# A two-block network on one core: softmax statistics in a tile for each branch, moved by SyncE; the tail's third tile loaded ahead of weights; a third store buffer

## The chip, the core and the metric

The kernel runs on one core of one Trainium2 chip. The metric is the device time of one execution in microseconds. Engines are named as in the profile: PE (TensorE), DVE (VectorE), ACT (ScalarE), POOL (GpSimd), SP (SyncE, which here only issues DMAs).

## The reference, cut to what matters

Two blocks, one after the other, on 2048 tokens of width 1024. The first has two layers, each with a Fourier mixer, a neighbourhood attention and a gated linear attention (GLA) side by side, and an output projection. The second is a dilated attention beside a gated MLP, an output product and a gated "ple" product:

```python
DILATIONS = ((128, 1), (512, 4), (2048, 16))
def _dilated_attention(q, k, v):                 # 8 heads of 64, 2048 tokens
    outs, lses = [], []
    for window, dilation in DILATIONS:
        o, l = _dilated_branch(q, k, v, window, dilation)   # banded softmax in blocks of 128
        outs.append(o)
        lses.append(l)                                      # m + log(den)
    w = softmax(stack(lses), axis=0)
    return sum(w[..., None] * stack(outs), axis=0)

def second_block(x, p, ...):
    ...
    o_b = _dilated_attention(q, k, v) * silu(gate_b)
    mixed = concatenate([o_b, o_a], axis=-1)                # o_a: gated MLP
    h = h + mixed @ w_out
    gate = sigmoid(_rmsnorm(h, g_ple) @ w_ple_gate + b_ple_gate)
    return h + gate * (p @ w_ple_proj)
```

The maximum m and the denominator den of each branch are per token; a branch of dilation r holds them in the order of its residue classes, so before the branches can be weighed against each other they have to be brought to one order.

## The kernel before

All products are in float32 made of two halves, hi and lo, with three products each (`split` makes the halves: hi on ACT, lo on DVE or POOL). The order of the instructions on each engine is made by a planner: it simulates the program with a cost model, takes instructions in program order where several are ready, and may pull later ones ahead; on the chip each engine then runs its list in order, and each waits for what it needs. In `b2_mid` SP's instructions keep the program's order from the end of the attention's units on (`tc.manual_schedule`).

**Dilated attention** (`b2_attn`, 3558 to 3935 us). Four pairs of heads; in each, three branches (`br` 0, 1, 2) of 16, 14 and 8 units (`n`); two units make a couple. `scores` computes a couple's scores (L1801, L1805), takes the row's extreme on DVE (L1812, into the column m of the statistics tile `ast`) and the Exp with its sum on ACT (L1814, into the column d). `turned` transposes (PE L1822, DVE L1824), `values` multiplies with V (L1838) and ACT stores into `aoT` (L1846); both run one and two couples behind. `gather` moves the statistics of branches 0 and 1 into the order of branch 2: a transpose on PE (L1854), a copy on DVE (L1857), one store `sd<-sts` (L1858) and four stores `sd<-ast` (L1861) to DRAM, and one load `ax<-sd` (L1864), all from POOL; it runs at units 1 and 4 of branch 2. `combine` begins with DVE's L1873, which reads `ax`, makes the weights on POOL (L1883 to L1894), stores them (`wd`, SP, L1895), loads them broadcast (`awb`, `awg`) and weighs and adds the three branches (L1924 to L1927: POOL for the first three pairs, mostly DVE for the last), and stores to `mixT` (L1930). In the program it begins in the next pair, but the planner pulls L1873 into branch 2. The operands of the next pair (`kq`, L1734, and `aV`, L1765 to L1770) are loaded on SP during a pair; 11 `kq` buffers serve five a pair.

**Tail** (`b2_mid`, `Tail`). For 16 tiles of 128 tokens: `products` (L2195, tile of `mixT` times `w_out`), `normed`, `turn` (transposes, L2236), `second` (L2254, times `w_ple_gate`). Weights go through raw buffers and are split. Tiles 0 and 1 have their buffers early, tile 2 gets the twelfth of the slots cut out of `kq` buffers and is loaded after the gate weights W6 and W7; W4, W5 and W0 to W3 of the gate go through two buffers `btr`.

**First block** (`mixers`). GLA steps run with gate units first; when these are done the neighbourhood attention's units (`na`) begin and one of them is drawn with each GLA step. What is left of them runs beside `ple_proj` (L1518 product, L1521 ACT copy into `plst`, L1522 store) and the output projection's weights. `OutProj.begin` then loads the first two tiles `om` (L1410); `products` splits a tile (`left`: `omh` on ACT, `om` on POOL) and multiplies (L1430).

## Time and profile before

| | us |
|---|---|
| median of 3 runs | 4350.35 (4340.16 to 4353.33) |
| the profiled execution | 4348.48 |
| its span | 4346.7 |
| PE busy | 4059.6 (93%) |
| DVE, ACT, POOL busy | 1738.6, 1642.4, 1501.5 |
| DMA, mean over the span | 145 GB/s |

1.8 us of the profiled execution lie outside the span. The mean granted clock of PE is 0.960 of full speed (of its two levels, 1.2 and 2.4 GHz). In a row of a timeline the columns are: start, duration, engine, line, instruction, written tile <- read tiles, shape, count, and in brackets the idle time of the engine just before and what ended it.

### The profile page before, as it was taken

To read this page: it belongs to the slowest core of one execution; us is meant where nothing else is said; L and a number is where in the kernel's file an instruction comes from. 1 tells how busy PE (TensorE), PEld (TensorE's weight loads), DVE (VectorE), ACT (ScalarE), POOL (GpSimd) and SP (SyncE) were. 2 spreads that over 40 slices of the span, in tenths; PEclk is the share of its full clock that TensorE was granted. 3 is DMA by queue.
4 is the path that set the end of the run, shared out by engine and by line. 5 is a ranking of instruction groups with operands and counts; after the bars stand their busy time and mean duration, and the time that the engine had idled before them with its cause. 6 is when DMAs were issued, how large, how long until landed. Compare 5 with 4: busy or idle time off the path is not lost. (4 is left out here: it accounts for less than half of the span.)

```text
span 4346.7 us, 79462 instructions
## 1 busy us (share of the span) xinstructions
PE 4059.6 (93%) x29633; PEld 3491.9 (80%) x29633; DVE 1738.6 (40%) x4996; ACT 1642.4 (38%) x4121; POOL 1501.5 (35%) x1949
## 2 busy tenths in 40 slices
PE   7999999898899999999988989989999989887998
PEld 6988789676677799888967767889998877765887
DVE  5331123477532443112347744544620036555222
ACT  5141233574551332323356554252222126553221
POOL 4234333224222323232321422445723332543433
PEclk9999999898999999999999989999999989888999
DMA  6435454766766444334477574532321267545231
GB/s 207 138 113 150 146 164 155 187 167 182 201 189 209 140 139 128 121 119 158 154 200 180 170 204 157 167 122 78 108 89 49 88 189 175 143 107 162 84 95 63
DMA packets 539035, 629.94 MB, mean 145 GB/s; under 512 B 118504, under 2 KB 417836, under 8 KB 535194
## 3 DMA queue, kind: packets, MB, share of 16 engines
q1 hardware_dynamic: 487546, 477.18, 38.7%
q0 software_dynamic: 39552, 129.60, 9.1%
q10 hardware_dynamic: 11552, 18.08, 1.2%
q8 instruction: 235, 3.85, 0.4%
q14 instruction: 150, 1.23, 0.1%
HBM read 424.26 MB, written 200.41 MB: 144 GB/s over the span
## 5 line engine op out<-in xcount | busy, mean ns | idle before, releaser
L301 PE MATMUL mm<-whi,hTh 128*128 128x304 f32 (+2 forms) x1424 | 420.3, 299 | 1.5 <-ACT hTh L221 1.5
L301 PE MATMUL mm<-wlo,hTh 128*128 128x304 f32 (+2 forms) x1424 | 417.7, 297 | 0.0
L301 PE MATMUL mm<-whi,hTl 128*128 128x304 f32 (+2 forms) x1424 | 381.1, 296 | 0.0
L254 POOL TENSOR_TENSOR wlo<-wraw,whi 128x128 fp32r<-128x128 f32 (+3 forms) x384 | 223.3, 608 | 404.2 <-ACT whi L253 392.1
L301 PE MATMUL mm<-whi,h2h 128*128 128x256 f32 x1024 | 293.1, 290 | 2.2 <-ACT h2h L221 2.2
L301 PE MATMUL mm<-wlo,h2h 128*128 128x256 f32 x1024 | 284.9, 282 | 0.0
L301 PE MATMUL mm<-whi,h2l 128*128 128x256 f32 x1024 | 271.9, 284 | 0.0
L301 PEld LDWEIGHTS mm<-whi,hTh 128*128 128x128 f32 x1424 | 269.1, 189 | 2.8 <-ACT hTh L221 2.0
L301 PEld LDWEIGHTS mm<-wlo,hTh 128*128 128x128 f32 x1424 | 268.9, 189 | 0.0
L301 PEld LDWEIGHTS mm<-whi,hTl 128*128 128x128 f32 x1424 | 257.0, 189 | 1.1 <-issue 1.1
L578 PE MATMUL gps<-gh,whi 128*128 128x256 f32 x816 | 233.4, 286 | 6.0 <-ACT gh L155 6.0
L578 PE MATMUL gps<-gh,wlo 128*128 128x256 f32 x816 | 232.2, 285 | 0.0
L578 PE MATMUL gps<-gl,whi 128*128 128x256 f32 x816 | 231.7, 284 | 0.0
L304 PE MATMUL mm<-hTh,whi 128*128 128x512 f32 x600 | 227.9, 381 | 0.0
L304 PE MATMUL mm<-hTh,wlo 128*128 128x512 f32 x600 | 227.0, 378 | 0.0
L304 PE MATMUL mm<-hTl,whi 128*128 128x512 f32 x600 | 226.4, 377 | 0.0
L1430 PE MATMUL ops<-owh,omh 128*128 128x512 f32 x544 | 215.1, 395 | 4.4 <-ACT omh L155 4.4
L1430 PE MATMUL ops<-owh,om 128*128 128x512 f32 x544 | 212.3, 391 | 2.0 <-POOL om L156 2.0
L1430 PE MATMUL ops<-owl,omh 128*128 128x512 f32 x544 | 212.5, 391 | 0.0
L1814 ACT ACTIVATE ae<-ae,ast 128x256 f32<-128x256 f32 (+1 forms) x384 | 171.1, 448 | 101.6 <-DVE ast L1812 101.6
L253 ACT ACTIVATE whi<-wraw 128x128 fp32r<-128x128 f32 (+3 forms) x416 | 127.3, 357 | 210.2 <-DMA wraw<-in_w_in 172.5
L301 PEld LDWEIGHTS mm<-wlo,h2h 128*128 128x128 f32 x1024 | 196.4, 192 | 0.0
(486 smaller groups left out, 10774.8 us busy)
## 6 DMA issues: line engine op xcount, KB each, us to landing
qkv<-gl SPq DMA_DIRECT2D x72, 384.0 KB
adaw<-in_w_ada SPq DMA_DIRECT2D x48, 512.0 KB
Q<-ql SPq DMA_DIRECT2D x88, 256.0 KB
hl<-evk SPq DMA_DIRECT2D x68, 256.0 KB
gl<-hl SPq DMA_DIRECT2D x17, 1024.0 KB
om<-mixTl SPq DMA_DIRECT2D x34, 512.0 KB
gTl<-ev POOLq DMA_DIRECT2D x67, 256.0 KB, 3.4
wraw<-in_w_in SPq DMA_DIRECT2D x32, 512.0 KB
```

The lines of the kernel that those rows point to most:

```text
L253: nc.scalar.activation(out=hi[:, :C], in_=raw[:, k], func=AF.Copy)
L254: (eng or nc.gpsimd).tensor_tensor(out=lo[:, :C], in0=raw[:, k], in1=f(hi[:, :C]), op=ALU.subtract)
L301: nc.tensor.matmul(ps[:, :C], s.hT[x][:, k, 128 * g:128 * g + 128], w[k][y][:, :C], start=st, stop=sp)
L304: nc.tensor.matmul(ps[:C, :tn], w[k][y][:, :C], s.hT[x][:, k, t0:t0 + tn], start=st, stop=sp)
L578: nc.tensor.matmul(ps.rearrange("p (t n) -> p t n", t=2), W[b][k][y][:, 128 * j:128 * j + 128], h[x][:, :, k], start=n == 0, stop=n == 23)
L1430: nc.tensor.matmul(ps, m[x][:, k], W[k][y][:, 512 * n:512 * n + 512], start=k == j == 0, stop=k == 7 and j == 2)
L1814: nc.scalar.activation(out=e, in_=e, func=AF.Exp, scale=-1.0, bias=m, accum_out=d)
```

## The change

Five edits. (1) The statistics are in one tile for each branch instead of one for all three; `gather` begins at unit 4 of branch 1 with its transpose, its copy and the store of branch 0 come at unit 8 of branch 1, the four stores of branch 1 at unit 2 of branch 2 and the load at unit 5; all its DMAs go from POOL to SP. (2) In the tail the third tile gets its buffer and its two loads right after the first step of weights; W6 alone goes through the old buffers, W7 and W4 go first through `btr`; the third tile is split on DVE at step 3. (3) `plst` has three buffers instead of two. (4) After the first `na` step the next three GLA steps draw no `na` unit; these come later, beside `ple_proj`. (5) `OutProj.first` splits tile 0 at the third of the `na` units that are left after `begin`, instead of in `products`.

```diff
--- before.py
+++ after.py
@@ -1347,13 +1347,16 @@
             left = 3 * ((54 if l == 0 else 48) + 2)
             for i, _ in enumerate(gla):
                 if units is not None:
-                    left -= 1
-                    next(units, None)
+
+                    if i > begun + 3:
+                        left -= 1
+                        next(units, None)
                 elif i % 3 == 2 and [x for x in range(2) if next(gates, 1)]:
                     e2.close()
                     keep.close()
                     units = na(K, A, l, S, B, pool(es, "na", side="right"), pp, (2, 3))
                     next(units)
+                    begun = i
                     pp.tile = pool(es, "naps", space=PSUM, side="right").tile
         next(w)
         with ExitStack() as e1:
@@ -1369,8 +1372,9 @@
                 for _ in x:
                     pass
         proj.begin()
-        for _ in units:
-            pass
+        for i, _ in enumerate(units):
+            if i == 2:
+                proj.first()
 
 
 
@@ -1399,8 +1403,12 @@
 
         s.p1 = s.es.enter_context(s.K.tc.tile_pool(name="opm", bufs=1, reuse_waits="tile"))
         s.ld = {}
+        s.m = {}
         for t in range(2):
             s.load(t)
+
+    def first(s):
+        s.m[0] = s.left(0)
 
     def load(s, t):
         if t >= len(s.tiles):
@@ -1471,7 +1479,7 @@
                 e1.close()
                 if s.ahead is not None:
                     s.ahead()
-            m = s.left(t)
+            m = s.m[t] if t in s.m else s.left(t)
             ps = []
             for n in range(2):
                 ps.append(pp.tile([128, 512], F32, name="ops", tag="ops"))
@@ -1489,7 +1497,7 @@
     W = (p.tile([128, 2, D], F32R, name="plwh"), p.tile([128, 2, D], F32R, name="plwl"))
     for c in range(4):
         cs = slice(256 * c, 256 * c + 256)
-        wr = p.tile([128, 2, 256], F32, name="plwr", tag="plst", bufs=2)
+        wr = p.tile([128, 2, 256], F32, name="plwr", tag="plst", bufs=3)
         nc.sync.dma_start(wr, A["w_ple_proj_2"][0][:, cs].rearrange("(k p) n -> p k n", p=128))
         split(K, W[0][:, :, cs], W[1][:, :, cs], wr)
     ld = {}
@@ -1517,7 +1525,7 @@
                 for a, b in MM3:
                     nc.tensor.matmul(ps, X[a][:, k], W[b][:, k, 512 * n:512 * n + 512], start=j == 0, stop=j == 5)
                     j += 1
-            o = p.tile([128, 512], F32, name="plst", tag="plst", bufs=2)
+            o = p.tile([128, 512], F32, name="plst", tag="plst", bufs=3)
             nc.scalar.activation(out=o, in_=ps, func=AF.Copy)
             nc.scalar.dma_start(ple[128 * t:128 * t + 128, 512 * n:512 * n + 512], o)
             yield
@@ -1783,7 +1791,7 @@
     def scores(pr, br, us, X):
 
 
-        st = X["st"]
+        st = X["st"][br]
         ps = [pp.tile([128, 2, 256], F32, name="aps", tag="aps", bufs=4) for _ in range(2)]
         ecs = [pa.tile([128, 2, 256], F32, name="ae", tag="ae", bufs=4) for _ in us]
         todo = []
@@ -1807,7 +1815,7 @@
             for hh in range(2):
 
                 col = (b, 4 * b + r, r)[br]
-                m, d = (st[:, br, x, hh, col:col + 1] for x in range(2))
+                m, d = (st[:, x, hh, col:col + 1] for x in range(2))
                 e = ecs[i][:, hh, cs]
                 nc.vector.tensor_tensor_reduce(out=e, in0=ps[hh][:, i, cs], in1=band[:, cs if full else slice(128, 256)], scale=1.0, scalar=BIG,
                                                op0=ALU.add, op1=ALU.min, accum_out=m)
@@ -1848,26 +1856,26 @@
     def gather(pr, X):
 
 
-
-        st = X["st"]
         pst = pp.tile([64, 128], F32, name="pst", tag="apo", bufs=2)
-        nc.tensor.transpose(pst, st[:, 0].rearrange("p s h t -> p (s h t)"), K.ident)
+        nc.tensor.transpose(pst, X["st"][0].rearrange("p s h t -> p (s h t)"), K.ident)
         yield
         sts = p.tile([64, 128], F32, name="sts", tag="sts", bufs=1)
         nc.vector.tensor_copy(sts, pst)
-        nc.gpsimd.dma_start(sd[pr, 0].rearrange("s h (t n) -> (s h t) n", n=128), sts)
+        nc.sync.dma_start(sd[pr, 0].rearrange("s h (t n) -> (s h t) n", n=128), sts)
+        yield
         for s_ in range(2):
             for hh in range(2):
-                nc.gpsimd.dma_start(dap(sd, ((pr * 2 + 1) * 4 + s_ * 2 + hh) * T, [[4, 128], [512, 4], [1, 4]]),
-                                  st[:, 1, s_, hh].rearrange("p (b r) -> p b r", r=4))
+                nc.sync.dma_start(dap(sd, ((pr * 2 + 1) * 4 + s_ * 2 + hh) * T, [[4, 128], [512, 4], [1, 4]]),
+                                  X["st"][1][:, s_, hh].rearrange("p (b r) -> p b r", r=4))
+        yield
         x = X["x"] = p.tile([128, 8, 16], F32, name="ax", tag="ax", bufs=1)
-        nc.gpsimd.dma_start(x, sd[pr].rearrange("b s h (i c) -> i (b s h) c", c=16))
+        nc.sync.dma_start(x, sd[pr].rearrange("b s h (i c) -> i (b s h) c", c=16))
 
     def combine(pr, X):
 
         oT = X["oT"]
         x = X["x"].rearrange("p (b s h) c -> p b s h c", b=2, s=2)
-        st = X["st"][:, 2:3]
+        st = X["st"][2].rearrange("p (o s) h t -> p o s h t", o=1)
         mn = p.tile([128, 32], F32, name="amn", tag="amn", bufs=1)
         m2 = mn.rearrange("p (h c) -> p h c", h=2)
         nc.vector.tensor_tensor(out=m2, in0=x[:, 0, 0], in1=x[:, 1, 0], op=ALU.min)
@@ -1956,10 +1964,11 @@
         X = Xs[pr]
         if n == 0:
             if br == 0:
-                X["st"] = p.tile([128, 3, 2, 2, 16], F32, name="ast", tag="ast", bufs=2)
-        if n == 0 and br == 2:
+                X["st"] = [p.tile([128, 2, 2, 16], F32, name="ast", tag="ast", bufs=6) for _ in range(3)]
+
+        if (br, n) == (1, 4):
             stat = gather(pr, X)
-        if br == 2 and n in (1, 4):
+        if (br, n) in ((1, 4), (1, 8), (2, 2), (2, 5)):
             next(stat, None)
         if n == 3 and br < 2:
             X["V"][br + 1] = load_v(pr, br + 1)
@@ -2095,18 +2104,19 @@
             for t in range(2):
                 tail.load(t, ((4, 8),))
             next(w)
+            tail.slots([slot()])
+            tail.load(2, ((4, 8),))
+            for t in range(3):
+                tail.load(t, ((0, 3),))
 
             def rest():
                 yield from w
                 ws = [slot() for _ in range(2)]
-                yield from tail.weights(tail.Wg, A["w_ple_gate_2"], tail.KG[:2], tail.raws,
-                                        lambda k: [ws[k - 6][:, D * i:D * i + D] for i in range(2)], nc.sync)
-                tail.slots([slot()])
-                for part in ((4, 8), (0, 3)):
-                    tail.load(2, (part,))
-                    tail.halves(2, (part,), nc.vector)
+                tail.W7 = ws[1]
+                yield from tail.weights(tail.Wg, A["w_ple_gate_2"], tail.KG[:1], tail.raws,
+                                        lambda k: [ws[0][:, D * i:D * i + D] for i in range(2)], nc.sync)
+                while True:
                     yield
-                yield from tail.gates()
 
             w2 = rest()
             i = 0
@@ -2120,12 +2130,16 @@
                     tail.halves(i, ((4, 8),))
                 if i == 2:
                     for t in range(2):
-                        tail.load(t, ((0, 3),))
                         tail.halves(t, ((0, 3),))
+                if i == 3:
+                    tail.halves(2, ((4, 8), (0, 3)), nc.vector)
+                next(w2)
                 if i == 10:
+                    while 6 not in tail.Wg:
+                        next(w2)
                     tail.hs = [tail.resid(t) for t in range(3)]
-                for _ in w2 if i == 10 else range(1):
-                    next(w2, None)
+                    for _ in tail.gates():
+                        pass
                 if i == 11:
 
                     for t in range(3):
@@ -2206,7 +2220,8 @@
     def gates(b):
 
         b.btr = [b.p1.tile([128, D], F32, name="btr", tag="tpl", bufs=2) for _ in range(2)]
-        yield from b.weights(b.Wg, b.A["w_ple_gate_2"], b.KG[2:3], b.btr, lambda k: [b.p1.tile([128, D], F32R, name=f"twg{k}{c}") for c in "hl"], b.K.nc.sync)
+        yield from b.weights(b.Wg, b.A["w_ple_gate_2"], b.KG[1:3], b.btr, lambda k: [b.W7[:, D * i:D * i + D] for i in range(2)] if k == b.KG[1]
+                             else [b.p1.tile([128, D], F32R, name=f"twg{k}{c}") for c in "hl"], b.K.nc.sync)
 
     def resid(b, t):
         h = b.p1.tile([128, D], F32, name="th", tag="th", bufs=3)
@@ -2265,7 +2280,7 @@
         b.ple, b.out = ple, out
         with b.es, tc.tile_pool(name="bt", bufs=1, reuse_waits="tile") as p, tc.tile_pool(name="btps", bufs=1, space=PSUM, reuse_waits="tile") as pp:
             hs = b.hs
-            for _ in b.weights(b.Wg, A["w_ple_gate_2"], b.KG[3:], b.btr[::-1], lambda k: [p.tile([128, D], F32R, name=f"twg{k}{c}") for c in "hl"], nc.sync):
+            for _ in b.weights(b.Wg, A["w_ple_gate_2"], b.KG[3:], b.btr, lambda k: [p.tile([128, D], F32R, name=f"twg{k}{c}") for c in "hl"], nc.sync):
                 pass
             b.bg = p.tile([128, D], F32, name="tbg")
             nc.sync.dma_start(b.bg, dap(A["b_ple_gate_2"], 0, [[0, 128], [1, D]]))
```

## Rows read from the trace of the kernel before

**Rows 1.** The page's part 4: the chain that ended last, shares by line.

```profile
PE mm L301 7%; PE mm L304 4%; PE tps L2195 3%; PE tps L2254 3%; DMA awb<-wd 1%; POOL aoT L1924 1%; POOL wlo L254 1%; PE apo L1838 0%; POOL gmo L2060 0%; PE apt L1822 0%; DMA awg<-wd 0%; POOL tpl L2260 0%; POOL tg L2259 0%; DMA ax<-sd 0%; ACT ae L1814 0%
```

**Rows 2.** Stretches of the attention: PE, PEld, DVE, ACT, POOL busy, clock, DMA, GB/s.

```profile
3600.00:3610.00 10.00, 10.00 (x86) 7.97 (x85) 7.15 (x29) 7.20 (x28) 0.00 (x0) 1.00 0.78 197
...
3720.00:3730.00 10.00, 0.00 (x0) 0.00 (x0) 0.00 (x0) 0.00 (x0) 4.87 (x8) 0.50 0.48 91
3730.00:3740.00 10.00, 5.57 (x34) 5.14 (x34) 6.19 (x37) 7.56 (x36) 0.00 (x0) 0.53 0.00 1
```

**Rows 3.** The tile `ax`: idle time until (us, times), and its landing.

```profile
  DMA ax<-sd: 57.1, 4
...
DMA to landing us min/median/max: 2.8/3.3/6.0
```

**Rows 4.** DVE's timeline, line L1873, pairs 0 to 3.

```profile
3635.96 0.19 DVE L1873 TENSOR_TENSOR amn<-ax 128x32 f32<-128x32 f32 x1 [8.49 <-DMA ax<-sd]
...
3730.43 0.19 DVE L1873 TENSOR_TENSOR amn<-ax 128x32 f32<-128x32 f32 x1 [19.39 <-DMA ax<-sd]
...
3827.55 0.19 DVE L1873 TENSOR_TENSOR amn<-ax 128x32 f32<-128x32 f32 x1 [22.32 <-DMA ax<-sd]
...
3925.97 0.19 DVE L1873 TENSOR_TENSOR amn<-ax 128x32 f32<-128x32 f32 x1 [6.90 <-DMA ax<-sd]
```

**Rows 5.** The tile `aps` on DVE (L1812): idle time until (us, times).

```profile
  PE aps L1805: 54.8, 48
```

**Rows 6.** ACT's timeline: last accumulator read of branch 1, pairs 0, 1 and 3.

```profile
3622.10 0.19 ACT L1814 ACTIVATION_READ_ACCUMULATOR ae<-ae,ast 128x1 f32 x1
...
3705.67 0.19 ACT L1814 ACTIVATION_READ_ACCUMULATOR ae<-ae,ast 128x1 f32 x1
...
3903.83 0.19 ACT L1814 ACTIVATION_READ_ACCUMULATOR ae<-ae,ast 128x1 f32 x1
```

**Rows 7.** POOL's timeline: the gather's DMAs in pair 0 and pair 1.

```profile
3620.98 3.00 POOL L1861 DMA_DIRECT2D sd<-ast  x4 [62.69 <-DVE ast L1812]
...
3629.96 0.94 POOL L1864 DMA_DIRECT2D ax<-sd  x1 [5.43 <-DMA sd<-sts]
...
3717.42 0.80 POOL L1861 DMA_DIRECT2D sd<-ast  x1
```

**Rows 8.** The tile `ast`: landing of its stores.

```profile
DMA to landing us min/median/max: 2.2/4.2/11.7
```

**Rows 9.** SP's timeline in pair 0, and SP's waits over the attention (total, times, longest).

```profile
3630.25 0.37 SPq L1765 DMA_DIRECT2D aV<-v  x1
...
SPq L1765 <- PE apo L1838: 76.5, 3, 30.1
```

**Rows 10.** Timelines at the start of the tail: PE, then ACT, SP and DVE.

```profile
3935.57 22.75 PE L2195 MATMUL tps<-tw,x 128*128 128x512 f32 x96
3971.60 1.22 PE L2195 MATMUL tps<-tw 128*128 128x512 f32 x2 [13.28 <-ACT tw L155]
...
3989.27 1.04 PE L2236 MATMUL tpt<-ident,ta 128*128 128x128 f32 x8
3993.45 0.96 PE L2254 MATMUL tps<-tw,tXh 128*128 128x512 f32 x3 [3.14 <-ACT tXh L155]
...
3970.91 1.07 ACT L155 ACTIVATE tw<-tw 128x512 fp32r<-128x512 f32 x2 [16.06 <-DMA tw<-mix]
...
3959.03 3.06 SPq L2174 DMA_DIRECT2D tw<-mix  x2
...
3977.41 0.74 DVE L2230 TENSOR_SCALAR ta<-th,tst 128x1024 f32<-128x1024 f32 x1
```

**Rows 11.** The line L1521 (`plst`): idle time of ACT until (us, times).

```profile
  DMA ple<-plst: 7.4, 1
```

**Rows 12.** A stretch at the start of `na`, layer 0; columns as in rows 2.

```profile
820.00:830.00 10.00, 8.45 (x78) 5.86 (x75) 4.52 (x14) 2.62 (x9) 3.25 (x5) 0.50 1.03 241
```

**Rows 13.** PE's timeline: first product of the output projection, layer 0.

```profile
1273.62 0.79 PE L1430 MATMUL ops<-owh,omh 128*128 128x512 f32 x1 [3.10 <-ACT omh L155]
```

## The prediction

> **What bounds the kernel now.** I read the page first: its chain of waits gives TensorE 19% of the span by name and DMA 3%, and among the DMAs that end waits it names `awb<-wd`, `awg<-wd` and `ax<-sd` [rows 1]. So the kernel is a TensorE kernel, and an edit pays only where TensorE stands still. The next view is busy time in stretches of 10 us over the attention of the second block (3558 to 3935 us). Its ordinary stretch has PE 10.00 of 10.00 at clock 1.00; in the third branch of a head pair there are stretches with PE at 0.00, and afterwards 5.57 at a clock of 0.53 [rows 2]. The view of the tile `ax` names the cause: VectorE waits 57.1 us in four waits for `ax<-sd`, the gathered statistics [rows 3], and the four L1873 rows of its timeline have 8.49, 19.39, 22.32 and 6.90 us [rows 4]. VectorE is in order, so the next scores (L1812) stand behind L1873, ScalarE's Exp behind those, and TensorE's transposes behind that. A couple of blocks waits 54.8/48 = 1.1 us for its scores anyway [rows 5], so the loss is 57.1 - 4 x 1.1 = **52.7 us**.
>
> Where do the 19 us of pair 1 come from? Call t0 the end of the last accumulator read of the second branch (ScalarE): 3622.3, 3705.9 and 3904.0 in pairs 0, 1 and 3 [rows 6]. VectorE begins to wait for x (start minus wait in rows 4) at t0 + 5.2, t0 + 5.2 and t0 + 15. GpSimd issues the first `sd<-ast` in pair 0 at once, but in pair 1 at 3717.42, 11.6 us after t0, since its own combine of the pair before is ahead of it; pair 2 repeats that. In pair 0, where GpSimd was free, x was issued at 3629.96, after 5.43 us for `sd<-sts`, and L1873 still lost 8.49 [rows 4, 7]. So there are two parts: the queue on GpSimd, and a chain of two DMAs that begins too late.
>
> **Statistics in a tile for each branch, moved by SyncE.** The first branch's transpose, copy and store go into the second branch: one instruction each on TensorE, VectorE and a queue, which are in the time of before as well, so they cost nothing more; what they depend on, the first branch, ended one branch earlier, so nobody waits there. The four `sd<-ast` and the x load go from GpSimd to SyncE. GpSimd spends 3.00 us on issuing four and 0.94 on x [rows 7]; SyncE's issue of an `aV` took 0.37 [rows 9]. New chain after t0: issue 4 x 0.37 = 1.5 to 3.0; landing 2.2 to 4.2 (minimum and median; 11.7 is the worst) [rows 8]; issue of x 0.4 to 0.9; landing of x 2.8 to 6.0 with a median of 3.3 [rows 3]. That is t0 + 6.9 to t0 + 14.1, and with middle values 2.2 + 3.5 + 0.6 + 3.3 about t0 + 10. Against t0 + 5.2, less the ordinary 1.1, pairs 0 to 2 lose 3.7 each; pair 3 (t0 + 15) loses nothing. 52.7 - 11 = 41.5, **-41 us**; the ends give -51 (0.6 each) and -29 (7.8 each). What is queued behind on SyncE: the next pair's `aV` and K/Q loads. SyncE stands for that `aV` anyway (76.5 us in three waits) and gets it in pair 0 at 3630.25, t0 + 8 [rows 9], so the small stores delay nothing by more than their issue; but if the x load falls behind `aV` it is issued at t0 + 8.4 and shares the engines with 1 MB, which is the 14.1 end again. GpSimd loses some 4.5 us of issue a pair, which its combine gains; no one waits for that in the third branch.
>
> The Trainium skill, page "DMA: Bandwidth & Descriptors", section "Issuing engines are not separate DMA queues", speaks against this move: DMAs of all issuing engines share the same 16 DMA engines, and another issuer saves only the sequencer's time, "usually small relative to the DMA itself". The trace does not agree for pair 1: what lies ahead of the store there is GpSimd's arithmetic, 11.6 us, and no DMA. Its result is the second rival below.
>
> **Clock.** The row behind the 19 us stall has PE busy 5.57 at 0.53: some 2.6 us lost at the lower of the two levels. Two long stalls lose 5.2 and two short ones less than that, 8 in all at most; as short stalls stay I take **-4** (0 to -8).
>
> **Tail, third tile.** TensorE ends tiles 0 and 1 at 3935.57 + 22.75 = 3958.3, begins tile 2 at 3971.60 with 13.28 us idle, and the gate product at 3993.45. ScalarE's split waited 16.06 us for `tw<-mix`, which SyncE issued at 3959.03 only [rows 10]. With the tile loaded ahead of the weights its 48 products (22.75/96 = 0.237 us each, 11.4) follow at once and end at 3969.7. Then the next late thing decides: `ta` of tile 0 stood at 3977.41 on VectorE, behind the combine of pair 3's second and third columns, and the gate product began 4.18 us after the transposes of `ta` (3989.27 to 3993.45) [rows 10]. `ta` ready at 3978 plus 1 for what lies between plus 4.2 makes about 3983, 10 us earlier. Against it: one more gate weight (W7) goes through the two buffers that W4, W5, 0 to 3 share, and the four loads of mix now stand on SyncE ahead of the `wd` store, which would be late if the last `mix` store of pair 2 were. I take **-8**; ends -2 (the weights eat it) and -18 (the `awb` and `awg` loads come earlier as well, with fewer bytes ahead).
>
> **Third store buffer.** One wait of `plst` for its store: 7.4 us [rows 11]. A third buffer removes it if the oldest store lands in the time of one more tile; -2 if most of the wait returns a tile later, -9 if TensorE keeps its clock as well. I take **-6**, since the view of the line has this one wait alone.
>
> **Neighbourhood attention three steps later, and the first split of the output projection.** Around the start of the neighbourhood units layer 0 has PE 8.45 at clock 0.50, with the DMA engines at 1.03 [rows 12]. Three GLA steps without these units in between give the loads time, but leave TensorE with GLA alone; the steps themselves move to the next stage. Nothing in the trace prices that: over two layers I take **-2**, between -16 (most of the idle time goes) and +16 (as much again is added). The split `omh`: TensorE waits 3.10 us for it in layer 0, but for a load that landed late, and less in layer 1 [rows 13]; earlier it may put ScalarE in front of an unlanded load. **0** (-3 to +4).
>
> Sum: -41 - 4 - 8 - 6 - 2 + 0 = -61. The profiled execution lasted 4348.5 us (span 4346.7), so 4287.5; the median of the runs is 1.9 us above that execution, which gives **4289 us**.
>
> **Rivals.** *x is still late on SyncE.* If the planner puts `aV` ahead of the `sd<-ast` stores, all of the chain begins at t0 + 8.4 and ends near t0 + 18: pairs 0 to 2 lose 11.7 each, pair 3 lost 3 - 1.1 = 2, so 37 of 52.7 stay. The attention gives -16, the clock nothing, the total with 8, 6 and 2 is -32: 4318. For it: three waits of SyncE for `aV` of up to 30.1 us [rows 9]. Against it: the stores are ready 8 us before `aV` is.
>
> *Only issue time is gained.* If the DMAs and not the queue were late, the gain would be GpSimd's 4.5 us less SyncE's 6 x 0.37 = 2.2 in each pair, 9 us, the total with 8, 6 and 2 is -25: 4325. Against it: pair 1's 11.6 us. This is the case that the Trainium skill's page would expect.
>
> *Slower.* Mechanism: the three GLA steps alone wait for their value loads behind the loads that the first neighbourhood step has already issued; TensorE idles and falls to the lower level, in both layers. It has to cost more than the rest brings: 59 + 13 = 72 us, 36 in each layer, where the stretch around the start lasts 50 now; with the first rival 30 + 13 = 43, 22 each. The rows show DMA engines at 1.03 there, which is for it; that the same loads are in flight now is against it.
>
> **How the numbers follow.** Forecast and its ends 0.66; x late on SyncE 0.15; only issue time 0.06; slower 0.08; the rest, about no change, 0.05. A measurement of this kernel tells some 0.3%, 13 us, from no change. Forecast, first rival and most of the second are faster: 0.82; same 0.10; slower 0.08. Range: the low end adds most of the bounds (-51 - 8 - 18 - 9 - 10 = -96, taken as -92), 4258; the high end covers the first two rivals and some of the unchanged cases, 4334.
>
> **What would show it.** Right: L1873's four waits fall to about 5, 5, 5 and 0 us, `sd<-ast` on SyncE within 3 us of t0, no stretch of the third branch with PE 0.00; the second tile's products run on into the third's at about 23 us after their start; the wait for `ple<-plst` is gone. Wrong: `ax<-sd` still above 30 us in sum; TensorE idle before tile 2 in the tail; the GLA stretch longer by tens of us in both layers; or a new wait of the next pair's first scores for K, Q or V.

## The result, and the profile after

The changed kernel takes 4293.91 us (median of 4 runs, 4285.62 to 4303.56) against 4345.26 for the kernel before (4 runs): a ratio of 0.9875 with a 95% interval of 0.9856 to 0.9895, so 46 to 63 us less. The forecast was 4289, with 4258 to 4334 as its range. The profiled execution of after is the fastest of its four (4285.62, span 4283.7), that of before one of the slower ones of its own, so a difference between the two traces alone (63 us) is somewhat too large; where it matters, the table below has the same stretch in several kernels.

First the statistics. The view of the tile `ax`, and VectorE's rows of L1881 (the L1873 of before), pairs 0 to 3, as in [rows 3, 4]:

```profile
  DMA ax<-sd: 14.3, 3
...
3615.30 0.18 DVE L1881 TENSOR_TENSOR amn<-ax 128x32 f32<-128x32 f32 x1
...
3689.38 2.19 DVE L1881 TENSOR_TENSOR amn<-ax 128x32 f32<-128x32 f32 x1 [7.00 <-DMA ax<-sd]
...
3770.93 0.19 DVE L1881 TENSOR_TENSOR amn<-ax 128x32 f32<-128x32 f32 x1 [2.57 <-DMA ax<-sd]
...
3856.99 1.50 DVE L1881 TENSOR_TENSOR amn<-ax 128x32 f32<-128x32 f32 x1 [4.71 <-DMA ax<-sd]
```

57.1 us of waiting became 14.3, where 15 were forecast. SyncE's timeline, the stores and the load of pairs 0 and 1, answers to [rows 7]:

```profile
3598.92 2.50 SPq L1868 DMA_DIRECT2D sd<-ast  x4
3608.50 0.36 SPq L1773 DMA_DIRECT2D aV<-v  x1
3609.04 0.99 SPq L1872 DMA_DIRECT2D ax<-sd  x1
...
3675.58 2.41 SPq L1868 DMA_DIRECT2D sd<-ast  x4
3685.47 0.36 SPq L1872 DMA_DIRECT2D ax<-sd  x1
3685.92 2.55 SPq L1773 DMA_DIRECT2D aV<-v  x1
```

In pair 1 the last accumulator read of branch 1 starts at 3675.81 on VectorE and at 3676.79 on ScalarE, and the four stores are issued from 3675.58 on, so they go out as the statistics appear, not 11.6 us later. But x is issued 9.9 us after the first store, and in pair 0 `aV` was ahead of it.

Busy time in stretches (columns as in [rows 2]): the whole attention, from the first to the last accumulator read of VectorE, before and after, and after the change a stretch behind the 7 us wait.

```profile
3552.90:3929.00 376.10, 319.93 (x2524) 263.47 (x2523) 219.00 (x935) 222.39 (x918) 147.87 (x171) 0.88 0.59 146
...
3532.80:3871.50 338.70, 319.46 (x2524) 261.21 (x2522) 221.74 (x935) 223.93 (x917) 130.49 (x147) 0.92 0.68 161
...
3690.00:3700.00 10.00, 4.66 (x30) 4.33 (x30) 7.52 (x37) 7.57 (x36) 6.86 (x8) 0.55 0.48 143
```

No stretch has PE at 0.00 any more; one with PE 4.66 at a clock of 0.55 is left. Over the attention PE is busy 319.46 us of 338.7; before it was busy 319.93 of 376.1. So idle time went, 56.2 to 19.2 us, and no busy time.

The tail: timelines of PE, then DVE and POOL, which answer to [rows 10].

```profile
3876.54 19.95 PE L2209 MATMUL tps<-tw,x 128*128 128x512 f32 x84
3906.55 4.97 PE L2209 MATMUL tps<-tw,x 128*128 128x512 f32 x12 [10.06 <-ACT x L155]
3911.36 11.04 PE L2209 MATMUL tps<-tw 128*128 128x512 f32 x48
3923.93 1.06 PE L2251 MATMUL tpt<-ident,ta 128*128 128x128 f32 x8 [1.54 <-DVE ta L2245]
3928.67 1.65 PE L2269 MATMUL tps<-tw,tXh 128*128 128x512 f32 x3 [3.67 <-ACT tXh L155]
...
3897.12 4.03 DVE L1932 TENSOR_TENSOR aoT<-aoT,awb 128x512 f32<-128x512 f32 x3 [8.36 <-DMA awb<-wd]
3901.18 1.63 DVE L1933 TENSOR_TENSOR aoT<-aoT 128x512 f32<-128x512 f32 x1
...
3909.68 0.69 DVE L1933 TENSOR_TENSOR aoT<-aoT 128x512 f32<-128x512 f32 x1
...
3902.35 1.59 POOL L1933 TENSOR_TENSOR aoT<-aoT 128x512 f32<-128x512 f32 x1
```

The third tile's 48 products now run on without a wait, but 10.06 us of idle time stand in front of the last 12 products of tiles 0 and 1 (their direct part), whose operand comes from the last pair's combine. The first gate product starts 57.2 us after the last score; before it was 64.5.

Before, those 12 products had no wait: the 96 ran on [rows 10], since the first column of the combine was ready early enough.

```profile
3950.03 1.90 DVE L1924 TENSOR_TENSOR aoT<-aoT,awb 128x512 f32<-128x512 f32 x3 [1.99 <-DMA awb<-wd]
...
3954.14 0.51 ACT L155 ACTIVATE x<-agt 128x128 fp32r<-128x128 f32 x2 [7.36 <-DVE agt L1927]
```

ScalarE could split it 25.1 us after the last score, and after the change only 34.7 us after it (3906.19). The `wd` store leaves 10.4 us after the last score instead of 7.7: GpSimd splits the operand x, whose load now comes earlier, for 2.45 us ahead of the weights (L1902). `awb` ends VectorE's wait at 25.6 instead of 21.0, and the first column takes 9.0 us instead of 4.1, since GpSimd's column now runs beside it.

The store buffers: in the view of `plst` ACT's waits for the store are gone, and only those for PE are left ([rows 11]).

```profile
  PE plo L1526: 13.3, 14
```

Where the time went, by stretches of the profiled executions, in us. "na" is from the last gate product (L578) to the last neighbourhood score (`sc`), "attention" as above, "tail" from there to the end; "ax" is VectorE's wait for it, and the last two columns are the median of the runs and the ratio, with its interval, to the runs of before that were made beside them (medians 4342 to 4345).

| kernel | na, layer 0 | na, layer 1 | attention | tail | ax | median | ratio |
|---|---|---|---|---|---|---|---|
| before | 467.0 | 448.7 | 376.1 | 417.7 | 57.1 | 4345.3 | |
| after | 458.7 | 437.5 | 338.7 | 412.2 | 14.3 | 4293.9 | 0.9875 (0.9856 to 0.9895) |
| s1_stats | 465.4 | 447.0 | 343.0 | 416.6 | 10.6 | 4316.2 | 0.9939 (0.9918 to 0.9960) |
| r1_order | 461.5 | 449.9 | 336.4 | 419.3 | 11.4 | 4309.4 | 0.9923 (0.9905 to 0.9941) |
| q1_sp | 467.6 | 453.3 | 347.0 | 417.0 | 24.9 | 4319.1 | 0.9949 (0.9930 to 0.9968) |
| q2_pool | 457.9 | 440.3 | 364.7 | 415.3 | 45.6 | 4317.9 | 0.9943 (0.9925 to 0.9960) |
| n1_na | 459.4 | 439.8 | 367.2 | 419.1 | 54.1 | 4330.9 | 0.9967 (0.9953 to 0.9981) |
| p1_plst | 461.1 | 441.9 | 376.1 | 416.8 | 58.2 | 4338.9 | 0.9986 (0.9971 to 1.0002) |
| f1_first | 463.2 | 451.3 | 368.4 | 415.9 | 54.4 | 4343.9 | 0.9996 (0.9978 to 1.0015) |
| t1_tail | 464.8 | 453.9 | 367.8 | 412.4 | 52.2 | 4342.0 | 0.9990 (0.9973 to 1.0006) |
| v3_order | 459.4 | 435.5 | 331.1 | 412.4 | 0 | 4278.7 | 0.9855 (0.9838 to 0.9873) |
| v2_tail | 459.0 | 439.9 | 337.8 | 409.9 | 12.9 | 4284.5 | 0.9867 (0.9851 to 0.9884) |
| v1_both | 460.9 | 438.0 | 334.8 | 411.6 | 0 | 4282.9 | 0.9863 (0.9847 to 0.9879) |
| n2_six | 461.6 | 445.2 | 343.6 | 412.4 | 19.7 | 4299.3 | 0.9908 (0.9892 to 0.9924) |

In s1_stats a third wait, of 6.1 us, stands at the same instruction, which the view puts down to GpSimd's L1925.

A stretch that a kernel doesn't touch scatters: layer 1 without the edit of the start of `na` or of the store buffers lies between 447.0 and 453.9, and the attention with the statistics of before (before, n1, p1, f1, t1) between 367.2 and 376.1, with a mean of 371.1. With the statistics of the change (after, s1, v2, n2) it has 338.7, 343.0, 337.8 and 343.6, a mean of 340.8. So the attention became some 30 us shorter, and the 37 of the two traces has some 7 us of chance in it. TensorE's idle time in it is 48.4 to 56.2 us in those five and 17.9 to 20.8 in these four.

### The profile page after: what moved, and what is told of

The parts are those of the page before. It is cut to its first block, busy times and chain, and to the rows that moved or that the text cites. A ratio compares the mean times of both kernels' runs of the same rounds, so it can differ in the third digit from the quotient of the medians.

```text
span 4283.7 us, 79449 instructions
## 1 busy us (share of the span) xinstructions
PE 4039.7 (94%) x29633; PEld 3474.4 (81%) x29633; DVE 1747.0 (41%) x4996; ACT 1645.8 (38%) x4121; POOL 1490.0 (35%) x1925
## 5 line engine op out<-in xcount | busy, mean ns | idle before, releaser
L301 PE MATMUL mm<-wlo,hTh 128*128 128x304 f32 (+2 forms) x1424 | 416.8, 296 | 0.0
L578 PE MATMUL gps<-gh,whi 128*128 128x256 f32 x816 | 233.9, 287 | 9.5 <-ACT gh L155 9.5
L578 PE MATMUL gps<-gh,wlo 128*128 128x256 f32 x816 | 232.5, 285 | 0.0
L578 PE MATMUL gps<-gl,whi 128*128 128x256 f32 x816 | 231.8, 285 | 0.0
```

The costliest lines, as they stand in the source:

```text
L301: nc.tensor.matmul(ps[:, :C], s.hT[x][:, k, 128 * g:128 * g + 128], w[k][y][:, :C], start=st, stop=sp)
L578: nc.tensor.matmul(ps.rearrange("p (t n) -> p t n", t=2), W[b][k][y][:, 128 * j:128 * j + 128], h[x][:, :, k], start=n == 0, stop=n == 23)
```

## The experiments

### The statistics alone, and the queue alone

s1_stats is the kernel before with the hunks of `scores`, `gather`, `combine` and the loop, and no others.

```diff
-    st = X["st"]
+    st = X["st"][br]
...
-    if br == 2 and n in (1, 4):
+    if (br, n) in ((1, 4), (1, 8), (2, 2), (2, 5)):
         next(stat, None)
```

> The kernel before with the statistics part of the change alone (a tile for each branch, moved in the second branch, all of it on SyncE). Theory A (VectorE's wait for the gathered statistics holds TensorE, and the change gains what it takes from that wait): the wait for ax falls from 57.1 us to about 15, the stretch from the first to the last score falls from 376 us to about 339, and the run is 37 to 42 us (0.85 to 0.97%) faster than before. Theory B (the gain of 54 us is spread over the first block, and the attention is worth no more than the issue time saved, 9 us): about 9 us faster.

Measured: 17 to 36 us faster (26.5 in the medians), the wait for `ax` 10.6 us, the attention 343.0. That is theory A in its mechanism and less than A in its size: B's 9 us are outside the interval, but so is A's 37.

q1_sp keeps the single tile and the old places in the program:

```diff
-        nc.gpsimd.dma_start(sd[pr, 0]..., sts)
+        nc.sync.dma_start(sd[pr, 0]..., sts)
...
-        nc.gpsimd.dma_start(x, sd[pr]...)
+        nc.sync.dma_start(x, sd[pr]...)
```

> The kernel before with the queue alone exchanged: the same single statistics tile and the same program places, all five stores and the load on SyncE. Theory A (the queue is most of it, the early store of branch 0 little): the wait for ax falls from 57.1 to 15 to 25 us and the run is 28 to 40 us faster than before. Theory B (moving the first branch's statistics one branch earlier is what counts): the wait stays above 35 us and the run is under 20 us faster.

The wait is 24.9 us, the attention 347.0, the run 23.5 us faster (14 to 30). In its wait theory A's; in its time between the two, as for s1_stats. The queue alone brings nearly all that the statistics part brings; the tile for each branch and the earlier store are worth 3 to 4 us more in these two runs, which their intervals don't tell from nothing.

q2_pool is the mirror image, the changed kernel with `nc.gpsimd` for `nc.sync` in `gather`:

> The changed kernel with its gather's DMAs issued from GpSimd again, at the program places of the change (store of branch 0 in branch 1, the rest at units 2 and 5 of branch 2). Theory A (GpSimd's queue made pairs 1 and 2 late): the wait for ax is back to 30 to 45 us, most of it in pairs 1 and 2, and the run is 15 to 30 us slower than the changed kernel. Theory B (only the time of issuing differs, some 2 us a pair): the wait stays under 22 us and the run within 9 us of the changed kernel.

The wait is back at 45.6 us, 36.8 of them in pairs 1 and 2 (VectorE's rows), and the run lies 24 us above the changed kernel by the medians and 30 by the ratios: theory A. POOL's timeline shows the order of pair 1 again: the four stores go out among its combine, from 3698.21 on.

```profile
3711.89 0.19 DVE L1881 TENSOR_TENSOR amn<-ax 128x32 f32<-128x32 f32 x1 [18.62 <-DMA ax<-sd]
...
3807.48 0.19 DVE L1881 TENSOR_TENSOR amn<-ax 128x32 f32<-128x32 f32 x1 [18.14 <-DMA ax<-sd]
...
3698.21 0.81 POOL L1868 DMA_DIRECT2D sd<-ast  x1
3700.26 0.80 POOL L1868 DMA_DIRECT2D sd<-ast  x1
3701.59 1.49 POOL L1868 DMA_DIRECT2D sd<-ast  x2
3708.48 0.90 POOL L1872 DMA_DIRECT2D ax<-sd  x1 [0.63 <-DMA sd<-ast]
```

So the rival "only issue time is gained" is out. Nor is it that a DMA from SyncE is much quicker: from the first store to the issue of x it takes 9.0 to 13.1 us before and 7.9 to 10.1 after the change. What went is what lay ahead of the first store: 11.6, 12.7 and 8.7 us after t0 in pairs 1 to 3 before, and 1.4 to 2.5 us ahead of t0 in all pairs after (t0 as in the prediction).

### The order of two operands

r1_order is the kernel before with this edit alone. Nothing is moved; the first minimum needs branch 2's own statistics, so it can't be placed in front of branch 2's scores.

```diff
-        nc.vector.tensor_tensor(out=m2, in0=x[:, 0, 0], in1=x[:, 1, 0], op=ALU.min)
-        nc.vector.tensor_tensor(out=m2, in0=m2, in1=st[:, 0, 0], op=ALU.min)
+        nc.vector.tensor_tensor(out=m2, in0=st[:, 0, 0], in1=x[:, 0, 0], op=ALU.min)
+        nc.vector.tensor_tensor(out=m2, in0=m2, in1=x[:, 1, 0], op=ALU.min)
```

> The kernel before with the two operands of the first minimum exchanged: branch 2's own statistics with x's first half, then the result with x's second half. The same work, the DMAs stay where and when they were on GpSimd; only, the first minimum needs the last score of the third branch, so the planner cannot put it in front of the third branch's scores on VectorE. Theory A (what costs is that VectorE stands in order at an instruction put too early, not that x is late): all of the 52.7 us is back apart from small waits, the run is 45 to 55 us (1.0 to 1.25%) faster, as much as the whole change or more than its statistics part. Theory B (x's lateness itself sets the end, since the combine waits for it): the wait moves to the combine on GpSimd and VectorE at the next pair, and the run is under 20 us faster.

Measured: 33 us faster (26 to 41), by the medians more than the whole statistics part (26.5, 17 to 36; the intervals overlap), with x as late as ever on GpSimd's queue: it is issued 9.3 to 13.4 us after the first store, 9.0 to 13.1 before. In three of the four pairs VectorE has no wait for `ax`. In pair 1 one of 11.4 us is left; L1873 stands there in front of the first scores of the next pair:

```profile
3731.09 0.19 DVE L1873 TENSOR_TENSOR amn<-ast,ax 128x32 f32<-128x32 f32 x1 [11.44 <-DMA ax<-sd]
...
3734.15 1.12 PE L1838 MATMUL apo<-aet,aV 128*64 128x128 f32 x8 [10.84 <-ACT aoT L1846]
```

That one wait is theory B's picture, the other three pairs are A's: x's lateness costs something where an instruction that needs it stands in front of scores. The size is between the theories, under A's 45 to 55: the attention has 336.4 us, 35 less than the mean of 371.1, where 44 of 55 us of waiting (the mean of the five kernels) went. v3_order and v1_both, below, have no such wait at all and 331.1 and 334.8 us, 38 less in the mean for all 55.

That is the missing term: a wait of VectorE doesn't cost TensorE its length, but some 0.7 of it here. In the profile of before the wait of 8.49 us, from 3627.47 to 3635.96, leaves PE this stretch:

```profile
3630.00:3640.00 10.00, 4.08 (x30) 3.67 (x28) 4.04 (x28) 3.58 (x19) 0.90 (x1) 0.85 0.69 164
```

5.9 us idle for 8.49: PE still has 6.5 us of work in the wait (the transposes and products of the couples behind), and stands for 4 us after it, until new work comes. For the four waits of 57.1 us together, each with the 6 us behind it, PE is idle 48.2 us, and outside them 8.0; v3_order, without such a wait, still has 12.5, so some of the idle time comes up elsewhere.

### The start of the neighbourhood attention

n1_na is the kernel before with the first hunk of the diff alone.

```diff
+                    if i > begun + 3:
-                    left -= 1
-                    next(units, None)
+                        left -= 1
+                        next(units, None)
```

> The kernel before with the start of the neighbourhood attention alone changed (three GLA steps without its units after the first). Theory A (the GLA steps get their loads and TensorE stands less at the start; this is what made layer 1's stretch from the last gate product to the last neighbourhood score 11 us shorter, 448.8 to 437.6): layer 1 is 7 to 11 us shorter, layer 0 up to 3, the run 8 to 14 us faster. Theory B (as predicted, about nothing: the stretch is shorter by the early split or by chance of the clock): under 4 us in either layer.

The run is 8 to 20 us faster (0.9967, 14 us in the ratio), layer 1's stretch 439.8 and layer 0's 459.4. In layer 1 that is 7 us below the shortest and 14 below the longest of the kernels without an edit there; in layer 0 (461.5 to 467.6 without) it is 2 to 8. So this edit, forecast at -2, is worth 14 us.

Why, the traces tell in part. The same number of products in layer 0 keeps TensorE busy for less time, and its idle time is the same (before, then n1_na; columns as in [rows 2]):

```profile
797.70:1264.70 467.00, 414.28 (x4539) 330.05 (x4538) 281.92 (x1018) 272.43 (x717) 129.47 (x176) 0.93 0.69 182
...
798.00:1257.40 459.40, 404.62 (x4539) 326.26 (x4538) 280.92 (x1018) 273.10 (x717) 130.41 (x176) 0.93 0.70 185
```

The seven kernels with this edit have 402.0 to 407.1 us of busy time there, the seven without it 410.6 to 417.3. In layer 1 it is mainly the idle time that is shorter, 50.5 us for 56.9. Waits for loads, theory A's cause, don't show it: over layer 1 VectorE waits for `bias` 8.5 us before and 9.2 in n1_na, and TensorE's wait for VectorE's L1195, 18.2 us before and 8.8 in n1_na, is 9.1 to 9.8 in s1_stats, t1_tail and p1_plst too, which haven't this edit. So the gain is shown and its cause stays open.

n2_six doubles the number of steps, in the changed kernel:

```diff
-                    if i > begun + 3:
+                    if i > begun + 6:
```

> The changed kernel with six GLA steps instead of three without the neighbourhood units at their start. Theory A (the first neighbourhood units stand for loads that are in flight, and GLA's own run meanwhile): further 2 to 5 us shorter in each layer (458.7 and 437.6 now). Theory B (three steps cover the loads; each further one is GLA alone, which leaves TensorE 25 to 35% idle for some 2.5 us a step): 0 to 5 us longer in each layer.

Layer 0 has 461.6 and layer 1 445.2 us, 2.9 and 7.7 longer; the run is at 0.9908. The other kernels with three steps have 457.9 to 460.9 and 435.5 to 440.3, so layer 0's difference is hardly clear of chance. That is theory B, with layer 1 beyond its 5 us: more than three steps bring nothing. (Its attention is longer as well, with 19.7 us of waits for `ax`, which the edit doesn't explain.)

### The third store buffer

p1_plst is the kernel before with `bufs=3` in the two `plst` lines.

> The kernel before with three store buffers in ple_proj alone. Theory A: the wait of ScalarE for the store, 7.4 us, goes, and layer 0's stretch from the last gate product to the last neighbourhood score falls from 467 to about 460; layer 1, which had no such wait, stays at 449. Theory B (the DMA engines are full there, so the wait comes back a tile or two later): a wait for the store of over 4 us remains, and layer 0 stays above 464.

One wait of ACT for the store is left, 4.0 us of 7.4:

```profile
  DMA ple<-plst: 4.0, 1
```

Layer 0 has 461.1, 4 us below the mean of the others without an edit there (464.9), the run is 6 us faster by its ratio, with an interval of -13 to +1. So neither theory whole: some of the wait came back. In the changed kernel, where the neighbourhood units lie differently, none did. Layer 1, with `ple_proj` as well but no wait for a store, has 441.9. From the first load `plwr`, where the edit begins to act, to the last score it takes 105.8 us there and 127.7 in layer 0; the six kernels without the edits in this stage take 109.1 to 111.2 and 130.4 to 132.4. So both layers are some 3 to 5 us shorter behind the edit, and the removed wait is not the whole reason. The edit gives the weights `plwr` a third buffer too, and the planner puts some of their splits earlier in both layers; whether that is the rest isn't shown.

### The early split

f1_first is the kernel before with `first` and its call.

> The kernel before with the early split of the output projection's first tile alone. Theory A (it hides the first split): TensorE's waits at the first product, 3.1 us in layer 0 and 1.3 and 1.6 in layer 1, fall by 1 to 4 us in sum, the run is unchanged within what can be measured. Theory B (ScalarE now stands at a load that has not landed, in front of the last neighbourhood units): the last scores come up to 4 us later.

The run is the same (0.9996). TensorE's waits at the first product didn't fall: in layer 0 3.90 where it was 3.10 [rows 13], in layer 1 1.31 and 1.60 as before.

```profile
1272.08 0.80 PE L1435 MATMUL ops<-owh,omh 128*128 128x512 f32 x1 [3.90 <-ACT omh L155]
...
1270.97 1.06 ACT L155 ACTIVATE omh<-om 128x1024 fp32r<-128x1024 f32 x1 [2.67 <-DMA om<-mixTl]
```

ACT waits for the load there, after all of the neighbourhood units, so being earlier in the program moves nothing: VectorE, ScalarE, GpSimd and SyncE run their instructions in the same order in the traces of both kernels. Neither theory's effect is seen. So f1_first also shows how far two executions of one order lie apart: 3.8 us in layer 0, 2.6 in layer 1, 7.7 in the attention.

### The tail

t1_tail is the kernel before with the hunks of `b2_mid` and `Tail` alone.

```diff
             next(w)
+            tail.slots([slot()])
+            tail.load(2, ((4, 8),))
+            for t in range(3):
+                tail.load(t, ((0, 3),))
```

> The kernel before with the tail's third tile loaded ahead of the weights, alone. Theory A: the stretch from the last score to the end falls from 417.7 by 4 to 8 us, as in the changed kernel (412.2), since TensorE's stand before the third tile only moves to the direct part of tiles 0 and 1, which waits for the combine. Theory B (that stretch was shorter in the changed kernel for another reason, the statistics' move or the clock): it stays within 2 us of 417.7.

The tail is 412.4 us, as in the changed kernel (415.9 to 419.3 in the kernels without the edit), the run 4 us faster (-12 to +3): theory A in the size. But the wait is not only moved: the direct part of tiles 0 and 1 had none before, and with this edit alone its operand is split 35.4 us after the last score, as in the changed kernel, instead of 25.1, and TensorE waits 8.9 us for it. v2_tail then asks what sets the rest, in the changed kernel:

```diff
             for x, y in ((4, 8), (0, 3), (3, 4)):
-                for t in range(2):
+                for t in range(3):
                     for n in range(2):
                         b.products(t, n, ps[t][n], x, y)
-            for n in range(2):
-                b.products(2, n, ps[2][n])
```

> The changed kernel with the third tile's products of the two loaded parts put ahead of the direct part of tiles 0 and 1. Theory A (TensorE's 10.06 us stand before the direct part only moved there from the third tile; the chain from the weights' store over awb, awg and VectorE's combine to the first gate product sets the end): the 10 us wait goes, but the first gate product starts within 3 us of where it does now after the last score (57 us), and the stretch to the end stays within 3 us of 412. Theory B (TensorE's order sets it): the first gate product comes 8 to 10 us earlier and the stretch falls to about 403.

```profile
3908.16 1.53 PE L2209 MATMUL tps<-tw 128*128 128x512 f32 x6
3920.30 1.94 PE L2251 MATMUL tpt<-ident,ta 128*128 128x128 f32 x8 [10.61 <-DVE ta L2245]
3925.38 2.08 PE L2269 MATMUL tps<-tw,tXh 128*128 128x512 f32 x4 [3.13 <-ACT tXh L155]
```

The 144 products end at 3909.7 instead of 3922.4, and TensorE then waits 10.61 us for VectorE. The first gate product comes 54.4 us after the last score instead of 57.2 (57.1 in v1_both, which has this edit too), the tail is 2.3 us shorter, which is within chance. That is theory A: what VectorE has to do up to `ta`, the last pair's combine in the main, sets the end of this stage, and TensorE's idle time only moves.

### What is left of the wait

v3_order is the changed kernel with the two operands exchanged as in r1_order, and v1_both has v2_tail's edit as well.

> The changed kernel with the exchanged operands of the first minimum as well. Theory A (the waits of 7.0, 2.6 and 4.7 us that the change left on VectorE still cost TensorE): no wait for ax on VectorE in the third branch, the attention's stretch falls from 338.7 to 330 to 335 us, the run is 4 to 9 us faster than the changed kernel (4285 to 4290 where that has 4294). Theory B (what is left is hidden): the stretch stays at 337 or above.

> The changed kernel with both, the exchanged operands and the third tile's products first. If the two are independent, the attention's stretch is that of the run with the operands alone and the tail's that of the run with the products alone; by theory A of both about 4284 to 4290, by theory B of the tail about 4277 to 4283.

v3_order has no wait for `ax` on any engine, an attention of 331.1 us and 4278.65 us in the median of four, 0.9855 of before and 15 us below the changed kernel's median, 9 by the ratios; its attention is 7.6 us shorter. Theory A. v1_both (4282.9) keeps the tail's stretch as it was (411.6), so the tail's edit adds nothing, and its interval covers v3_order's ratio. By its median v3_order is the fastest of all.

## Why the prediction was right

The sum was -61 and the measured change -46 to -63, but not all terms were right. The parts alone add up: 0.61 + 0.10 + 0.33 + 0.14 + 0.04 = 1.22% against 1.25 for the whole, each with an interval of some 0.15 to 0.2 to either side.

**What bounds the kernel.** Right: VectorE stood at L1873, in order, and the scores behind it. r1_order shows it without moving a DMA, and behind the one wait that is left there TensorE stands for 10.84 us.

**Attention, -41, and the clock, -4.** The waits were forecast at 5, 5, 5 and 0 and came at 0, 7.0, 2.6 and 4.7, 14.3 in sum for 15. The time they gave back was mis-sized: the stretch is about 30 us shorter in the mean of several kernels, and s1_stats is 26.5 us faster. The step that failed is "loss = wait - 1.1 us": VectorE's ordinary wait was subtracted, but not the work that TensorE still has when VectorE stops, so 55 us of waits cost about 38 and not some 51. Of the clock's term nothing is seen: TensorE's busy time in the attention is the same before and after. The chain came as it was drawn: VectorE has x at t0 + 12.4, 8.6 and 8.7 in pairs 1 to 3, for a forecast of about t0 + 10 between 6.9 and 14.1, though x was issued at t0 + 8.5 in pair 1, for a forecast of about 6. What was wrong is when VectorE begins to wait: at t0 + 14.3 in pair 0, where x is there already, and at t0 + 4.0 in pair 3, where nothing was to be lost. These two make up for each other in the sum, which is luck. `aV` ahead of x, named as a danger, happened in pair 0 and cost nothing, since VectorE comes to L1881 only at 3615.30 there.

**Tail, -8.** 4 to 6 us. That the third tile follows without a wait was right; that the next late thing is `ta`, behind the combine on VectorE, was right too (v2_tail). What wasn't seen: with the loads of mix earlier, the last pair's combine comes 9 to 10 us later after the last score, so that the direct part of tiles 0 and 1, ahead of the third tile in TensorE's order, gets a wait that it didn't have. The `wd` store behind those loads was named as a danger; it leaves 2.7 us later, for GpSimd's split and not for a store of `mix`.

**Third buffer, -6.** 6 us in the ratio, with zero just inside the interval; in the changed kernel the wait is gone. The term counted that wait alone, which is in layer 0; as much of the gain is in layer 1, so the number is right for more than the reason given.

**Start of the neighbourhood attention, -2 between -16 and +16.** -14, near the end of its range. The forecast took the middle because no row prices the start. The rows did show the DMA engines full and TensorE at a half of its clock [rows 12]; that three steps without new units give the loads time was named, but not weighed, and the runs don't show that this is the reason.

**First split, 0.** Right, for the reason given: the load is late.

So an attention that, with the clock, was some 15 us too high and a start that was 12 too low made up for each other: that the sum came so close is luck, while the mechanism of the largest term is right. The rivals: x late on SyncE would have left 37 us of waits, and 14.3 are left; only issue time gained is contradicted by q2_pool; the slower case, GLA steps starved by the loads, didn't come; six steps (n2_six) cost some us, but whether by the loads isn't shown.

## What to carry to other kernels

When an engine waits in order for something late, look first at whether the waiting instruction has to stand where it does: exchanging two operands, so that it depends on what comes last anyway, gave at least as much as the whole rebuilt transport. Price a wait by the idle time of the bounding engine in the stretch, not by the length of the wait on another engine. And before you count a removed wait in TensorE's order as gained, ask which engine ends the stage, and whether the same edit makes that engine later: in this tail it was VectorE's combine, and of 13.28 us of idle time that the edit took away 10.06 came up elsewhere.

## What the runs showed of the hardware

A 128x512 addition of float32 on VectorE takes 0.69 us alone and 1.63 beside one of GpSimd's, and GpSimd's takes 1.59 there instead of about 1.28 in the attention: the rows of the tail above, at 3901.18, 3909.68 and 3902.35, and the durations (minimum, median, maximum) of its 36 in the attention of the changed kernel:

```profile
L1932 POOL TENSOR_TENSOR aoT<-aoT,awb x36: 1265/1280/1305, 3650.8 to 3857.2; 128x512 f32<-128x512 f32 x36
```

The Trainium skill, page "SBUF — State Buffer", section "SBUF: two separate sides", says that VectorE with two SBUF inputs and GpSimd hold a shared pair of ports in turn, each for a whole instruction. The trace agrees in that both run at one pace, about 1.6 us for a pair of instructions; that is less than 0.69 + 1.28, so here they aren't wholly one after the other. In this tail VectorE's first column takes 9.0 us for it, ahead of the direct part. In the kernel before GpSimd's column ran beside VectorE's second, from 3959.28 on, and the first took 4.1 us; no run takes GpSimd's column out of the way of both.
